# Moving the heads' beta products to VectorE, the convolutions one block later, and the last weight forms one block earlier in a one-core decoder layer

## The chip, the cores and the metric

The kernel runs on one NeuronCore of a Trainium2 chip. The metric is device time in microseconds (us) of one execution, and lower is better. TensorE (PE) multiplies matrices, VectorE (DVE) and ScalarE (ACT) work on elements, GpSimd (POOL) does some elementwise work and issues the stores that the code calls `store`, and SyncE (SP) issues all other transfers.

## The reference

One layer on x of shape 1 x 1024 x 1024 (sequence by channels), all in float32, with a conditioning vector c that gives shift, scale and gate:

```python
h = rmsnorm(x, pre_mix_g) * (1 + sc1) + sh1
glu_in, qkv, gates = split(h @ w_in)
# branch A: u = u_val * sigmoid(u_gate); causal depthwise conv of 31 taps over 512 channels;
#           layernorm, silu, projection
# branch B: stick-breaking attention, 8 heads of 64
z = q @ k.T / 8
log_keep = where(causal, log_sigmoid(-z), 0)
log_after = reverse_cumsum(log_keep) - log_keep
a = where(causal, exp(log_sigmoid(z) + log_after), 0);  o = a @ v
y = (sigmoid(g_conv) * y_conv + sigmoid(g_att) * y_att) @ w_o
x = x + ga1 * rmsnorm(y, post_mix_g)
h = rmsnorm(x, pre_ffn_g) * (1 + sc2) + sh2
gate, up = split(h @ w_ffn_in);  y = (silu(gate) * up) @ w_ffn_out      # 2816 wide
x = x + ga2 * rmsnorm(y, post_ffn_g)
```

## The kernel before

**Layout.** Activations lie with the channels on the 128 partitions. A float32 product is made of three fast ones: each operand is split into a rounded part hi and a rest lo, and hi*hi, hi*lo and lo*hi are added in PSUM. So every operand costs one copy on ScalarE (L158) and one subtraction on VectorE.

**Order.** The program's text gives each instruction a priority. A planner walks a clock of its own costs and puts the ready instruction of the best priority next on its engine; `tc.high_priority(offset=n)` moves a block n places ahead, a negative offset moves it back. On the chip each engine takes its instructions in the order so fixed. Tiles come from pools with a number of buffers for each tag, and a new tile waits until the buffer's last tile is done with, a store that reads it included. Pools open on a stack: a pool that opens after another has closed lies on the same memory, and its tiles wait for the tiles that lay there.

**The mixing stage.** For p = 0 to 3 the text has `glu(p)` (the gate and value products of 128 convolution channels; their product u is written to DRAM as `v_d`), `conv(p)` and `attend(p)` (heads 2p and 2p+1). `conv(p)` reads `v_d` back in another arrangement into `ph` (one buffer), loads five 512 KB tiles `cvw` of weights into the three `wraw` buffers that all raw weights share, and makes 80 products of 128 x 128 by 128 columns (L361). Before this change `conv(3)` stands behind the loop, together with the gate products that are left. `attend(p)` has high priority; `qk_pair(p+1)`, the next heads' queries and keys, stands between its two heads. So TensorE fills the gaps of the heads with whatever stands behind them in the text and has its data.

**A head** takes 12 steps. One step: scores z on TensorE (L451, L452, and L454 for the mask); two sigmoids on ScalarE, kap of -z (L455) and beta of z (L456); a running product over kap from the right on VectorE (L459); beta times the running product on GpSimd (L461); then the 128 x 128 blocks are transposed on TensorE (L471), split by ScalarE (L474) and VectorE (L475), and multiplied with v (L480, L481). Over 8 heads there are 96 steps, 48 of them 512 wide and 16 each of 384, 256 and 128.

**The FFN's first half** runs over 22 column blocks f in a pool `pv`, with tags `y2` (8 buffers of 4 KB a partition) and `wt` (9 of 2 KB). A block has seven products of 12 matmuls each on TensorE; for f under EARLY = 11 two of them were made earlier. Its results go out with two stores from `y2` tiles to `g_d` (names p and uw). For f in W2_AT, `w2_forms` also makes sums of four quarters of a second-half weight, splits them, and stores them to `w_d`: four loads, four sums and four rests on VectorE, four copies on ScalarE, four `y2` tiles and four 512 KB stores on GpSimd's queue.

**The FFN's second half** opens `pg` on the memory where `pv` lay. Its tag `gt` (5 buffers) holds the split operands of the first sweep `pa`: ScalarE's copy of X (L158, gb) writes into such a buffer, and TensorE's first products (L1397) read it.

Of the kernel before, what the change touches and what calls it, by code (L numbers as in the profile page):

```python
# [10 lines left out]
F32 = mybir.dt.float32  # L11
# [3 lines left out]
ALU = mybir.AluOpType  # L15
# [3 lines left out]
P = 128  # L19
# [3 lines left out]
CH = 512  # L23
# [27 lines left out]
EARLY = 11  # L51
TLATER = 40
CORDER = [(0, 1, 2, 3)] * 6 + [(3, 2, 1, 0)] * 2
FH = FT // 2
# [3 lines left out]
AHEAD = 2  # L58
FIN_AT = (8, 8)
DOT_AT = "pb"  # L60
W2_AT = tuple(range(EARLY, EARLY + FH))
W2_LATER = 100
W_S3, W_S1, W_S2, W_S4 = range(4)

# [10 lines left out]
def tile_block(ctx: ExitStack, tc: tile.TileContext, xT, vecs, crow, ada1, ada2, win, wv, wcv, wat, wo, w1, w2, cvw, out):  # L75
    nc = tc.nc
    act, dve, pool, pe = nc.scalar, nc.vector, nc.gpsimd, nc.tensor

    def mkpool(stack, name, bufs=1, **kw):
        return stack.enter_context(tc.tile_pool(name=name, bufs=bufs, reuse_waits="tile", **kw))  # L80
# [21 lines left out]
    def load(dst, src):  # L102
        nc.sync.dma_start(dst, src)
# [85 lines left out]
    def bank(name):  # L189
        return psm.tile([P, CH], F32, tag="main", name=name)  # L190
# [6 lines left out]
    with ExitStack() as s0:  # L197
# [48 lines left out]
        with tc.high_priority(offset=2 * SOONER):  # L246
            for c in range(NCH):
                m, a = (p0.tile([P, CH], F32, tag="nr", name=f"nr{c}{i}", bufs=4) for i in range(2))
# [69 lines left out]
    with ExitStack() as sC:  # L318
        pc = mkpool(sC, "pc")
        with ExitStack() as sA:  # L320
# [25 lines left out]
            def conv(ct):  # L346
                ph = pc.tile([P, NG, SH - 1 + TM], F32, tag="ph", name=f"ph{ct}", bufs=1)
                pool.memset(ph[:, :, 0:SH - 1], 0.0)
                load(ph[:, :, SH - 1:], v_d[ct].rearrange("g p m -> p g m"))
                wts = []  # L350
                for hf in range(2):
                    cv = bank(f"pcv{ct}_{hf}")
                    o = sgp.tile([P, NG // 2, TM], F32, tag="sg", name=f"co{ct}_{hf}", bufs=2)
                    for gi in range(NG // 2):
                        g = hf * (NG // 2) + gi
                        for d in range(SH):
                            n, at = divmod((g * SH + d) * P, T)
                            if n == len(wts):
                                wts.append(wp.tile([P, T], F32, tag="wraw", name=f"cvw{ct}_{n}"))
                                load(wts[n], cvw[ct, n])  # L360
                            pe.matmul(cv[:, gi * TM:(gi + 1) * TM], wts[n][:, at:at + P],  # L361
                                      ph[:, g, SH - 1 - d:SH - 1 - d + TM], start=(d == 0), stop=(d == SH - 1))
                    for gi in range(NG // 2):
                        b = C_CB + ct * NG + hf * (NG // 2) + gi
                        act.activation(o[:, gi], cv[:, gi * TM:(gi + 1) * TM], AF.Identity, bias=vec[:, b:b + 1],
                                       scale=1.0)
                    load(u_d[ct][hf * (NG // 2):(hf + 1) * (NG // 2)].rearrange("g p m -> p g m"), o)
# [54 lines left out]
            def head(p, hh, qst, kst, klo, vts, oT):  # L422
# [3 lines left out]
                tag = f"{p}_{hh}"  # L426
                av = None
                order = CORDER[2 * p + hh]
                for ci, c in enumerate(order):
                    if ci % 2 == 0:  # L430
                        av = psv.tile([P, CH], F32, tag="av", name=f"av{tag}_{c}")
                    avc = av[:, (c % 2) * 256:(c % 2) * 256 + 256]
                    kaps = {}
                    nsc = 1 if c < 2 else 2
                    for sc in range(nsc - 1, -1, -1):
                        probs = []
                        for i in (2 * c, 2 * c + 1):
                            W = P * (i + 1)
                            if i not in kaps:
                                kaps[i] = pa.tile([P, T], F32, tag="kap", name=f"ka{tag}_{i}", bufs=2)  # L440
                            kap = kaps[i]
                            s_lo, s_hi = sc * CH, min(W, (sc + 1) * CH)
                            w = s_hi - s_lo
                            beta = pa.tile([P, CH], F32, tag="beta", name=f"be{tag}_{i}_{sc}", bufs=4)
                            tcols = slice(i * P, (i + 1) * P)
                            z = psz.tile([P, CH], F32, tag="z", name=f"z{tag}_{i}_{sc}")
                            z_lo = s_lo if w >= 256 else max(0, s_hi - 256)
                            z_hi = max(s_hi, z_lo + 256)
                            zw, zo = z_hi - z_lo, s_lo - z_lo
                            diag = s_hi == W  # L450
                            pe.matmul(z[:, :zw], qst[:, tcols], kst[:, z_lo:z_hi], start=True, stop=False)  # L451
                            pe.matmul(z[:, :zw], qst[:, tcols], klo[:, z_lo:z_hi], start=False, stop=not diag)  # L452
                            if diag:
                                pe.matmul(z[:, zo + w - P:zo + w], identb, mask, start=False, stop=True)  # L454
                            act.activation(kap[:, s_lo:s_hi], z[:, zo:zo + w], AF.Sigmoid, bias=0.0, scale=-0.125)  # L455
                            act.activation(beta[:, :w], z[:, zo:zo + w], AF.Sigmoid, bias=0.0, scale=0.125)  # L456
                            rev = kap[:, s_lo:s_hi][:, ::-1]
                            init = 1.0 if diag else kap[:, s_hi:s_hi + 1]
                            dve.tensor_tensor_scan(rev, rev, rev, init, op0=ALU.mult, op1=ALU.bypass)  # L459
                            m = w - 1 if diag else w  # L460
                            pool.tensor_tensor(beta[:, :m], beta[:, :m], kap[:, s_lo + 1:s_lo + 1 + m], op=ALU.mult)  # L461
                            probs.append(beta)
                        for jp in range(min(c, 2 * sc + 1), 2 * sc - 1, -1):
                            tr = pst.tile([P, CH], F32, tag="tr", name=f"tr{tag}_{c}_{jp}")
                            for jj in range(2):
                                j = 2 * jp + jj
                                for ii in range(2):
                                    jo = (j - 4 * sc) * P
                                    src = zeros if (jp == c and jj == 1 and ii == 0) else probs[ii][:, jo:jo + P]
                                    o = jj * 256 + ii * P  # L470
                                    pe.transpose(tr[:, o:o + P], src, ident)  # L471
                            ahi = pa.tile([P, CH], F32R, tag="ahi", name=f"ahi{tag}_{c}_{jp}", bufs=2)
                            alo = pa.tile([P, CH], F32R, tag="alo", name=f"alo{tag}_{c}_{jp}", bufs=2)
                            act.activation(ahi, tr, AF.Copy)  # L474
                            dve.tensor_tensor(alo, tr, ahi, op=ALU.subtract)  # L475
                            for jj in range(2):
                                j = 2 * jp + jj
                                lhs = vts[j][:, hidx].rearrange("p a d -> p (a d)")
                                cols = slice(jj * 256, jj * 256 + 256)
                                pe.matmul(avc, lhs, ahi[:, cols], start=(jp == c and jj == 0), stop=False)  # L480
                                pe.matmul(avc, lhs, alo[:, cols], start=False, stop=(jp == 0 and jj == 1))  # L481
                    if ci % 2 == 1:
                        cs = slice((c // 2) * CH, (c // 2 + 1) * CH)
                        act.activation(oT[half, cs], av[other], AF.Copy)
                        dve.tensor_tensor(oT[half, cs], av[half], oT[half, cs], op=ALU.add)
# [16 lines left out]
            for p in range(4):  # L502
                glu(p)
                if p == 2:
                    v = v_half(1)
                if p < 3:
                    conv(p)
                qk = attend(p, qk, v)
            conv(3)
            for n in PLAIN:  # L510
# [21 lines left out]
    with ExitStack() as sG:  # L532
        pg = mkpool(sG, "pg")
# [228 lines left out]
    with ExitStack() as sF:  # L762
# [592 lines left out]
        for f in range(PIN, FT):  # L1355
            raw_w(f)
            for _ in ffn(f):
                pass
            if f in W2_AT:
                with tc.high_priority(offset=-W2_LATER):  # L1360
                    w2_forms(W2_AT.index(f))

    with ExitStack() as sG:
        pg = mkpool(sG, "pg")
        psg = mkpool(sG, "psg", 4, space=PSUM)

# [4 lines left out]
            return hp.tile([P, 2, CH], dt, tag="act", name=name)  # L1371

        def x_tile(name):
            return pg.tile([P, 2, CH], F32, tag="xr", name=name, bufs=4)

        def bank(name):
            return psg.tile([P, CH], F32, tag="main", name=name)
# [175 lines left out]
        c22 = out_tiles("c22", (h_tile, g_tile))  # L1553
        b2 = sweep("pa", prep1, (True, True))
        c11 = out_tiles("c11", (x_tile, x_tile))
        for n in range(NH):
            act.activation(c11[n], ka[n], AF.Copy)
# [131 lines left out]
```

## Time and profile before

| | |
|---|---|
| median of 3 runs (lowest to highest) | 1438.71 us (1438.03 to 1440.59) |
| the profiled execution: its own time | 1440.23 us |
| its span in the trace | 1438.2 us |
| TensorE busy | 1384.5 us, 96% of the span |
| VectorE busy | 1020.9 us, 71% |
| ScalarE busy | 653.8 us, 45% |
| GpSimd busy | 195.4 us, 14% |
| mean DMA rate | 180 GB/s |

Busy is time with at least one instruction in the engine. Matmuls overlap one another, so a stage in which TensorE is shown as fully busy can still differ in how many matmuls it gets done; the counts tell that.

### The profile page before, as it was taken

The numbers are of one execution on the slowest core, as the hardware profiler recorded it, in microseconds if no ns is written. First come the engines' busy times: TensorE is split into PE (matmuls) and PEld (weight loads), VectorE is DVE, ScalarE is ACT, GpSimd is POOL, SyncE is SP. The second block draws the span as 40 slices with busy tenths as digits, with TensorE's granted clock in tenths as the row PEclk, the third lists the DMA queues.
The fourth block names the chain that finished last, engine by engine and source line by source line (L and its number), as shares of the span: only waits on it lengthen the run. The fifth ranks groups of instructions, "written<-read, shape, count | busy, mean of one in ns | idle before, by whom it ended". The sixth has DMA issues, their size and how long they took to land.

```text
span 1438.2 us, 18913 instructions
## 1 busy us (share of the span) xinstructions
PE 1384.5 (96%) x6882; PEld 1159.7 (81%) x6882; DVE 1020.9 (71%) x1496; ACT 653.8 (45%) x1136; POOL 195.4 (14%) x279
## 2 busy tenths in 40 slices
PE   4999999999999999999999999999999998999996
PEld 4888888898888777788877778888888886888886
DVE  7686466546576789779579878777787786785357
ACT  6275456436463447413356543333444443433441
POOL 0033042412230111000011100001111111000000
PEclk9999999999999999999999999999999999999998
DMA  9211304113043563784934535445677789588833
GB/s 382 88 45 59 132 30 147 44 60 118 22 156 103 192 210 126 274 300 142 359 117 160 185 138 179 158 146 180 221 259 252 238 285 393 182 316 294 282 120 117
DMA packets 91260, 259.25 MB, mean 180 GB/s; under 512 B 9760, under 2 KB 20128, under 8 KB 90144
## 3 DMA queue, kind: packets, MB, share of 16 engines
q1 hardware_dynamic: 75232, 203.52, 41.3%
q0 software_dynamic: 15936, 54.54, 10.1%
q8 instruction: 54, 0.88, 0.2%
q14 instruction: 38, 0.31, 0.1%
HBM read 191.43 MB, written 66.58 MB: 179 GB/s over the span
## 4 chain that ended last, share of the span: by engine, by line
PE 52%; issue 26%; DMA 7%; DVE 7%; POOL 4%; ACT 2%; SPq 0%; POOLq 0%; DVEq 0%; ACTq 0%
PE ka L1397 8%; PE pwo L790 6%; PE pb L1397 4%; PE pg L179 3%; PE pgv L179 3%; PE pv L381 3%; PE pcv L361 3%; PE pgg L179 2%; PE pq L179 2%; PE pk L179 2%; PE pa L1397 2%; PE tr L471 2%; PE ka L315 2%; POOL w_d L106 2%; POOL g_d L106 2%
## 5 line engine op out<-in xcount | busy, mean ns | idle before, releaser
L461 POOL TENSOR_TENSOR be<-be,ka 128x127 f32<-128x127 f32 (+2 forms) x96 | 99.9, 1053 | 234.1 <-DVE ka L459 120.5
L459 DVE TENSOR_TENSOR_SCAN ka<-ka 128x128 f32<-128x128 f32 (+2 forms) x96 | 95.2, 1015 | 40.1 <-ACT ka L455 40.0
L475 DVE TENSOR_TENSOR alo<-tr,ahi 128x512 fp32r<-128x512 f32 x80 | 53.3, 684 | 43.8 <-ACT ahi L474 43.3
L455 ACT ACTIVATE ka<-z 128x128 f32<-128x128 f32 (+2 forms) x96 | 47.7, 498 | 55.2 <-PE z L454 36.3
L474 ACT ACTIVATE ahi<-tr 128x512 fp32r<-128x512 f32 x80 | 46.5, 603 | 44.3 <-PE tr L471 32.0
L1397 PE MATMUL ka<-gt,w2f 128*128 128x512 f32 x264 | 63.4, 389 | 0.7 <-DMA w2f<-w_d 0.7
L1397 PEld LDWEIGHTS ka<-gt,w2f 128*128 128x128 f32 x264 | 49.5, 188 | 11.3 <-issue 1.0
L975 PE MATMUL ke<-b,w_hi 128*128 128x512 f32 x176 | 55.1, 394 | 0.0
L134 DVE SCALAR_TENSOR_TENSOR ada<-ada,cb 128x1024 f32<-128x1024 f32 x32 | 38.9, 1222 | 19.3 <-DMA ada<-in_ada_dram 19.2
L456 ACT ACTIVATE be<-z 128x128 f32<-128x128 f32 (+2 forms) x96 | 47.3, 501 | 6.0 <-PE tr L471 5.9
L471 PE MATMUL tr<-ident,be 128*128 128x128 f32 x288 | 49.2, 273 | 0.7 <-DVE alo L475 0.4
L480 PE MATMUL av<-ahi,vst 128*128 128x256 f32 x160 | 44.7, 294 | 1.9 <-ACT be L456 1.2
L481 PE MATMUL av<-alo,vst 128*128 128x256 f32 x160 | 43.2, 296 | 2.1 <-DVE alo L475 1.9
L106 POOL DMA_DIRECT2D g_d<-uw x22 | 11.9, 542 | 245.0 <-DVE uw L1288 245.0
L361 PE MATMUL pcv<-ph,cvw 128*128 128x128 f32 x320 | 42.8, 276 | 1.2 <-DMA ph<-v_d 1.2
L361 PEld LDWEIGHTS pcv<-ph,cvw 128*128 128x128 f32 x320 | 39.7, 192 | 2.1 <-DMA ph<-v_d 1.1
L1397 PE MATMUL ka<-gb,wa 128*128 128x512 f32 x132 | 33.0, 398 | 6.8 <-ACT gb L158 6.8
L975 PEld LDWEIGHTS ke<-b,w_hi 128*128 128x128 f32 x176 | 33.0, 188 | 7.7 <-issue 1.0
L381 PE MATMUL pv<-wv_hi,hhi 128*128 128x256 f32 x128 | 37.1, 290 | 1.4 <-DVE qst L405 0.8
L158 ACT ACTIVATE gt<-X 128x512 fp32r<-128x512 f32 x33 | 20.4, 629 | 38.9 <-PE ka L1397 11.6
L471 PEld LDWEIGHTS tr<-ident,be 128*128 128x128 f32 x288 | 35.0, 140 | 2.6 <-POOL be L461 1.1
L381 PE MATMUL pv<-wv_hi,hlo 128*128 128x256 f32 x128 | 36.5, 285 | 0.0
(525 smaller groups left out, 4128.8 us busy)
## 6 DMA issues: line engine op xcount, KB each, us to landing
w_d<-w2o POOLq DMA_DIRECT2D x44, 512.0 KB, 7.5
w2f<-w_d SPq DMA_DIRECT2D x44, 512.0 KB, 5.4
ada<-in_ada_dram SPq DMA_DIRECT2D x32, 512.0 KB, 5.4
w2r<-in_w_dram SPq DMA_DIRECT2D x44, 256.0 KB, 3.9
w1g<-in_w_dram SPq DMA_DIRECT2D x21, 512.0 KB, 3.6
w1u<-in_w_dram SPq DMA_DIRECT2D x21, 512.0 KB, 4.7
cvw<-in_cvw_dram SPq DMA_DIRECT2D x20, 512.0 KB, 3.6
ada_w<-in_ada_dram SPq DMA_DIRECT2D x8, 1024.0 KB, 12.7
```

The costliest lines, as they stand in the source:

```text
L106: nc.gpsimd.dma_start(dst, src)
L179: pe.matmul(bank, st[:, cols], mv[k][:, c * CH:(c + 1) * CH], start=(i == 0 and s == 0), stop=(i == n - 1 and s == 2))
L361: pe.matmul(cv[:, gi * TM:(gi + 1) * TM], wts[n][:, at:at + P], ph[:, g, SH - 1 - d:SH - 1 - d + TM], start=(d == 0), stop=(d == SH - 1))
L381: pe.matmul(pv[:, :256], st[k][:, tcols], mv[:, wc], start=(k == 0 and i == 0), stop=(k == KT - 1 and i == 2))
L455: act.activation(kap[:, s_lo:s_hi], z[:, zo:zo + w], AF.Sigmoid, bias=0.0, scale=-0.125)
L459: dve.tensor_tensor_scan(rev, rev, rev, init, op0=ALU.mult, op1=ALU.bypass)
L461: pool.tensor_tensor(beta[:, :m], beta[:, :m], kap[:, s_lo + 1:s_lo + 1 + m], op=ALU.mult)
L471: pe.transpose(tr[:, o:o + P], src, ident)
L475: dve.tensor_tensor(alo, tr, ahi, op=ALU.subtract)
L790: pe.matmul(bank_, st[:, cols], mv[k][:, cs], start=(k == 0 and q == 0), stop=(k == KT - 1 and q == 2))
L975: pe.matmul(kbs[f], wes[f][st][:, cols], t[:, mv], start=(i == 0 and j == 0 and q == 0), stop=(j == HK - 1 and q == 2), skip_group_check=i ...
L1397: pe.matmul(dst, w[st][:, cols], g[mv], start=first and s == 0, stop=last and s == 2, skip_group_check=more)
```

## The change

There are three edits. Beta's product moves from `pool` to `dve`. `conv(p)` for p below 3 moves from beside the heads of its own block to beside those of the next, so that `conv(2)` stands with the last pair of heads and `conv(3)` still behind the loop. At the FFN's border `w2_forms` runs for f = 10 to 20 in place of 11 to 21, and the tag `xr` (4 buffers of 4 KB a partition, used from the end of the first sweep on) gets a pool `px` of its own, which opens ahead of `pg`.

```diff
-W2_AT = tuple(range(EARLY, EARLY + FH))
+W2_AT = tuple(range(EARLY - 1, EARLY - 1 + FH))
...
-                            pool.tensor_tensor(beta[:, :m], beta[:, :m], kap[:, s_lo + 1:s_lo + 1 + m], op=ALU.mult)
+                            dve.tensor_tensor(beta[:, :m], beta[:, :m], kap[:, s_lo + 1:s_lo + 1 + m], op=ALU.mult)
...
                 glu(p)
                 if p == 2:
                     v = v_half(1)
-                if p < 3:
-                    conv(p)
+                if p:
+                    conv(p - 1)
                 qk = attend(p, qk, v)
             conv(3)
...
     with ExitStack() as sG:
+        px = mkpool(sG, "px")
         pg = mkpool(sG, "pg")
...
         def x_tile(name):
-            return pg.tile([P, 2, CH], F32, tag="xr", name=name, bufs=4)
+            return px.tile([P, 2, CH], F32, tag="xr", name=name, bufs=4)
```

## Rows read from the trace of the kernel before

**Rows 1.** The page's first two parts: engines, and TensorE in 40 slices.

```profile
PE 1384.5 (96%) x6882; PEld 1159.7 (81%) x6882; DVE 1020.9 (71%) x1496; ACT 653.8 (45%) x1136; POOL 195.4 (14%) x279
...
PE   4999999999999999999999999999999998999996
...
PEclk9999999999999999999999999999999999999998
```

**Rows 2.** TensorE's waits over the whole span: total, times, longest.

```profile
PE pvar L245 <- DVE rstd L238: 17.7, 1, 17.7
PE ka L1397 <- ACT gb L158: 6.8, 1, 6.8
...
PE av L481 <- DVE alo L475: 1.9, 2, 1.5
...
PE pcv L361 <- DMA ph<-v_d: 1.2, 2, 0.9
```

**Rows 3.** Stretches around the FFN's border: busy us by engine, clock, DMA.

```profile
core 0: us, PE busy (x) PEld busy (x) DVE busy (x) ACT busy (x) POOL busy (x), PEclk, DMA share, GB/s
...
960.00:1000.00 40.00, 40.00 (x178) 33.13 (x177) 30.93 (x50) 14.11 (x24) 3.23 (x6) 1.00 0.47 154
1160.00:1200.00 40.00, 40.00 (x178) 33.14 (x177) 30.79 (x49) 19.34 (x35) 6.45 (x12) 1.00 0.91 326
1180.00:1225.00 45.00, 38.24 (x162) 31.14 (x161) 29.53 (x47) 17.54 (x32) 4.32 (x8) 0.92 1.04 394
1200.00:1240.00 40.00, 33.24 (x140) 27.00 (x139) 27.09 (x44) 14.97 (x27) 1.09 (x2) 0.91 0.85 319
```

**Rows 4.** The chain of waits across the border, 1194 to 1212 us.

```profile
1194.63 12.30 DMA w_d<-w2o
...
1207.01 0.64 ACT gb L158
1207.64 0.04 issue
1207.69 2.08 PE ka L1397 x4
```

**Rows 5.** Stretches of the mixing stage, columns as in rows 3.

```profile
60.00:480.00 420.00, 412.67 (x2526) 360.49 (x2525) 261.05 (x332) 221.57 (x451) 111.03 (x112) 1.00 0.26 83
120.00:140.00 20.00, 18.19 (x123) 15.49 (x122) 15.68 (x19) 12.24 (x25) 8.70 (x8) 1.00 0.19 64
200.00:220.00 20.00, 18.62 (x135) 16.56 (x134) 15.45 (x20) 12.43 (x28) 8.91 (x9) 1.00 0.25 79
380.00:400.00 20.00, 17.34 (x111) 14.72 (x110) 13.37 (x18) 10.78 (x26) 7.56 (x9) 1.00 0.15 52
82.00:138.00 56.00, 53.52 (x377) 47.50 (x376) 41.53 (x54) 33.43 (x77) 23.17 (x23) 1.00 0.09 29
365.00:425.00 60.00, 57.28 (x374) 50.25 (x373) 41.53 (x50) 36.21 (x81) 23.43 (x23) 1.00 0.28 94
```

**Rows 6.** The chain of waits at the first convolution.

```profile
129.45 2.61 DMA v_d<-u
...
132.12 3.94 DMA ph<-v_d
136.05 0.14 issue
136.19 2.25 PE pcv L361 x18
```

**Rows 7.** SP's issues behind that store, in order of time.

```profile
138.24 3.04 SPq L103 DMA_DIRECT2D cvw<-in_cvw_dram  x2
...
144.44 0.41 SPq L103 DMA_DIRECT2D wq_raw<-in_win_dram  x1
```

**Rows 8.** Groups by shape: beta's product on POOL, VectorE's nearest products.

```profile
L461 POOL TENSOR_TENSOR be<-be,ka 128x512 f32<-128x512 f32 x32 | 42.3, 1335 | 70.8 <-ACT be L456 40.8 <-DVE ka L459 21.7 <-ACT ahi L474 2.5
...
L1288 DVE TENSOR_TENSOR uw<-uw 128x512 f32<-128x512 f32 x22 | 15.1, 687 | 1.6 <-ACT uw L1287 1.2
```

**Rows 9.** The last stores of the FFN's first half, GpSimd's queue.

```profile
1192.82 2.34 POOL L106 DMA_DIRECT2D w_d<-w2o  x4 [4.16 <-DVE w2o L878]
1200.62 0.54 POOL L106 DMA_DIRECT2D g_d<-uw  x1 [5.46 <-DVE uw L1288]
1201.95 0.55 POOL L106 DMA_DIRECT2D g_d<-p  x1 [0.78 <-DVE p L1296]
```

**Rows 10.** Stores between 1150 and 1220 us: KB each, median us to landing.

```profile
w_d<-w2o POOLq DMA_DIRECT2D x12, 512.0 KB, 8.4
...
g_d<-p POOLq DMA_DIRECT2D x4, 256.0 KB, 5.2
```

**Rows 11.** ScalarE's copies of the sweep's weights, from the timeline.

```profile
1223.34 0.63 ACT L158 ACTIVATE wa<-wa 128x512 fp32r<-128x512 f32 x1 [4.78 <-DMA wa<-in_w_dram]
```

## The prediction

> **What bounds the kernel now.** I read the page's engine table first: TensorE is busy 96% of the span, and in the 40 slices only the first, the last and one near the five-sixths mark fall short of 9 [rows 1]. So TensorE's work sets the time, and an edit that leaves that work as it is can win only TensorE's gaps. The list of its waits then says where the gaps are: 17.7 us at the start, which no edit touches, one of 6.8 us at L1397, and then small ones of under 2 us [rows 2]. The change touches two places, and for each I took the stretches around it.
>
> At the FFN's border a full stretch of 40 us holds 178 matmuls; the one from 1200 holds 140, with a granted clock of 0.91 [rows 3]. The chain of waits names the cause: the last `w_d` store takes 12.30 us to land, only then does ScalarE write the first gb, and TensorE starts 0.68 us after that; its first four matmuls take 2.08 us [rows 4], where full stretches need 40/178 = 0.225 us each. So gb's buffer lies on a weight form that is still being stored.
>
> In the mixing stage, from 60 to 480 us, TensorE is idle for 420 - 412.67 = 7.3 us. Three stretches of 20 us hold 1.8 + 1.4 + 2.7 = 5.9 of them [rows 5]. The first is a round trip: u goes to DRAM in 2.61 us, comes back as `ph` in 3.94 us, and the convolution starts 6.7 us after the store did [rows 6]. The second has the same shape. In the third the last pair of heads runs out of other work while `conv(3)` waits for its `ph`.
>
> **The border, part by part.** Removed: `w2_forms` after f = 21. The forms of its weight go out one block earlier, 84 matmuls or 84 x 0.225 = 18.9 us, so that their four stores, issued from 1192.82 on [rows 9], are issued near 1174; with the 12.30 us of [rows 4] the last has landed by about 1190, and TensorE reaches the border at 1201. What is late next: only the last block's two `g_d` stores, issued at 1200.62 and 1201.95 [rows 9], which hold 2 of the 8 `y2` buffers and land about 5.2 us later [rows 10]. With `px` first, `pg` begins 16 KB further on, so that `gt`'s five buffers lie on the upper four `y2` buffers and on `wt` tiles, which nothing stores. An operand that lies on such a `g_d` tile comes free near 1201.95 + 0.55 + 5.2 = 1207.7. If it is one of the later of the five, this costs nothing or little, as one operand serves 12 matmuls, or 2.7 us. I take the whole gap as gone: 178 - 140 = 38 matmuls at 0.225 us, -8.5 us; this has both the idle 6.8 us and the slow matmuls behind it. Bounds: 0 (the first operand lies on a `g_d` tile) and -8.5.
>
> The Trainium skill (Trace Analysis, section Identifying the Most-Contended Engine) calls busy matmul time a bad measure of what TensorE has left and wants the weight loads' busy share. By it the border costs 40 x (1 - 27.00/33.14) = 7.4 us [rows 3], against 8.5 us by the count; I keep the count.
>
> Added: a form block at f = 10, which has five products in place of seven, 60 x 0.225 = 13.5 us. VectorE works 30.93 of 40 us there [rows 3], 10.4 us in such a block, and the form adds eight instructions of about 0.69 us (by the nearest shape [rows 8]), 5.5 us: 2.4 us more than the block has. The form has the lower priority and the next block, of 18.9 us, has 18.9 x (1 - 30.79/40) = 4.4 us free with its own form counted in, so I take 0; uncovered it is +2.4 us.
>
> The transfers: from 1180 to 1225 the DMA engines are full, at 394 GB/s [rows 3], and the sweep's weights are late, with ScalarE waiting 4.78 us for one until 1223.34 [rows 11]. That one serves the fifth step; at 24 matmuls a step TensorE would want it near 1201 + 4 x 5.4 = 1222.6, some 8 us sooner than now. But the four stores of 0.52 MB leave this stretch, 2.1/0.394 = 5.3 us of it, so it lands near 1218, and with a copy and a rest (1.3 us) it is ready with 3 us to spare. Price 0; if the stores don't move out of the way, about +2 to +3 us.
>
> **Beta on VectorE.** POOL loses 96 products; 32 of them, 512 wide, take 1.335 us each [rows 8]. VectorE gains them. Its nearest row is the product of two SBUF tiles of that width, 0.687 us [rows 8]. Upper bound: 96 x 0.687 = 66 us. Lower: by columns, the mean width being 383, 96 x 0.687 x 383/512 = 49 us. I take 55, since narrow instructions keep some of their fixed time. All of it lies beside TensorE's work: VectorE is busy 261 of the 420 us [rows 5], and 316 still fits. A pair of heads gains 24 products, 12 to 16.5 us; in the two tightest stretches VectorE has 56 - 41.5 = 14.5 and 60 - 41.5 = 18.5 us free [rows 5]. That is close in the first. A step gets shorter by a handover and by about 1.3 - 0.7 = 0.6 us. On TensorE's path I take 0.
>
> The Trainium skill (VectorE: DVE Perf Modes, section on the trn2 errata) gives a float32 tensor_tensor of N columns (N + 151)/0.96 ns, a fixed cost per instruction that speaks against 96 more of them; by it an estimate is 54 us. Its 691 ns at 512 agrees with the row's 687; no row here has the narrow widths on VectorE.
>
> **The convolutions.** Nothing is added: per block one `ph` load, five `cvw` loads, two `u_d` stores and 80 matmuls move behind `glu(p+1)`. On SP's queue the `cvw` loads no longer stand ahead of the next query weights, which today are issued at 144.44, behind the first convolution's waits [rows 7]; so the query and key products can fill the first pair of heads at once, and each later pair finds a convolution whose `ph` can have been there for long. Of the 5.9 us in the three stretches, I take -4. Bounds: -7.3 (all of the stage's idle time), and a loss: `conv(3)` now follows `conv(2)` directly with one `ph` buffer, so its load of 3.94 us [rows 6] can start only when `conv(2)` is through. The heads that are left and the transfer's start hide it, else +3.9 us.
>
> **Sum.** -8.5 - 4 = -12.5 us against the profiled execution's own 1440.23 us (span 1438.2, 2.0 around it): 1427.7. That execution lies 1.5 us above the median shown, so the median to expect is 1426.2, say 1426.
>
> **The rivals.**
> (a) Likeliest, as above, chance 0.55. Its own range takes the convolutions from -7.3 to 0: 1423 to 1430.
> (b) The border wins, the mixing stage doesn't: the `ph` handover or VectorE's longer queue gives back what the round trips cost, net up to +3.9. Around 1433. Speaking for it: one `ph` buffer, and VectorE 78% busy in 120 to 140 before the products come. Chance 0.15.
> (c) The first gb lies on a late `g_d` tile: it comes at 1207.7 in place of 1206.9, nothing is won there, and -4 is left: 1434.7. Against it: two late buffers of eight, and `px` moves the first operands' place. Chance 0.13.
> (d) The wait goes and a transfer takes its place, +3 at the sweep's fifth step: 1429. Chance 0.05.
> (e) Slower: VectorE becomes the heads' bound. Place: the four pairs of heads. It decides if the free time of a pair can't be used because the running products and the splits wait in order for ScalarE. If half of it is usable, the tight pairs lack 16.5 - 7.2 and 16.5 - 9.2 us, 17 in all, and TensorE stands for it once its other work is out: 1438.7 - 8.5 + 17 = 1447. Against it: TensorE has other work for most of that time. Chance 0.07.
> (f) The planner's new order puts as many waits elsewhere as it takes away, about 1438.7. Chance 0.05.
>
> **How the numbers follow.** About 0.2% (2.9 us) is what a measurement of this kernel can tell from no change. Faster means below 1435.8: (a), (b), (d) and nearly half of (c), 0.81. Same: the rest of (c) and (f), 0.12. Slower: (e), 0.07. The range runs from 1420, the full 7.3 us in the mixing stage and some 3 us by a better order behind it, to 1437, the upper side of (c); above lie (e) and (f).
>
> **What would show it.** Right: no wait of L1397 on gb near 1190 to 1210, a full 178 matmuls in each 40 us there and a granted clock of 1.00; L461 on DVE at 0.5 to 0.7 us; L361 with no wait on `ph`; 4 us less idle from 60 to 480. Wrong: gb waiting on a `g_d` store; TensorE waiting on VectorE's running product or beta's product in the heads; a wait on `ph` between `conv(2)` and `conv(3)`.

## The result, and the profile after

The changed kernel takes 1420.48 us (median of 4 runs, 1418.78 to 1421.85) against 1439.28 us before, a ratio of 0.987 with a 95% interval of 0.9854 to 0.9885: 18.8 us less. That is faster, as forecast, but 5.5 us below the forecast of 1426: outside the 1423 to 1430 of rival (a) and just inside the lower end of the whole range, 1420. The profiled execution took 1418.78 us, with a span of 1417.0 us.

The page's engines and slices after, with the group of beta's product:

```profile
PE 1376.3 (97%) x6882; PEld 1155.8 (82%) x6882; DVE 1061.4 (75%) x1592; ACT 653.0 (46%) x1136; POOL 96.3 (7%) x183
...
PE   4999999999999999999999999999999999999996
...
PEclk8999999999999999999999999999999999999999
...
L461 DVE TENSOR_TENSOR be<-be,ka 128x127 f32<-128x127 f32 (+2 forms) x96 | 53.3, 572 | 9.7 <-ACT be L456 5.0
```

The gap near the five-sixths mark [rows 1] is gone. TensorE's number of matmuls is the same, POOL has lost 96 instructions and VectorE has gained them: 53.3 us of busy time in all. VectorE's own busy time rose by less, from 1020.9 to 1061.4 us. In part its instructions overlap, and in part others became shorter: the running products of 128 columns (L459) took 541 ns on average before and 418 after. TensorE's waits after (total, times, longest):

```profile
PE pvar L245 <- DVE rstd L238: 17.0, 1, 17.0
...
PE ka L1398 <- ACT gb L158: 1.2, 1, 1.2
...
PE pcv L361 <- DMA ph<-v_d: 0.9, 1, 0.9
```

L1397 of before is L1398 here, as the pool `px` adds a line. Its wait on gb has shrunk from 6.8 us [rows 2] to 1.2 us. The chain of waits across the border after:

```profile
1184.72 2.73 PE ka L867 x12
...
1187.48 0.02 ACT wa L158
...
1188.02 0.62 ACT gb L158
...
1188.68 1.19 PE ka L1398 x4
```

No store stands in it any more, where before the chain ran through a 12.30 us store [rows 4]. After TensorE's last product of the first half ScalarE makes one copy of a weight (wa) and then gb:

```profile
1187.48 0.63 ACT L158 ACTIVATE wa<-wa 128x512 fp32r<-128x512 f32 x1 [1.36 <-PE ka L867]
1188.02 2.70 ACT L158 ACTIVATE gb<-X 128x512 fp32r<-128x512 f32 x5
```

The sweep's first four matmuls take 1.19 us in place of 2.08. Two 40 us stretches at the border after (columns as in [rows 3]):

```profile
1160.00:1200.00 40.00, 38.76 (x172) 31.77 (x171) 26.89 (x43) 16.87 (x30) 4.30 (x8) 1.00 1.00 371
...
1200.00:1240.00 40.00, 40.00 (x178) 33.15 (x177) 28.16 (x44) 15.74 (x27) 0.00 (x0) 1.00 0.57 199
```

The granted clock stays at 1.00, the upper level of 2.4 GHz, after an idle time of 1.2 us; before it was 0.91 over 40 us after 6.8 us idle [rows 3]. The stretch behind the border holds its full 178 matmuls. The mixing stage after:

```profile
60.00:480.00 420.00, 417.36 (x2559) 366.16 (x2558) 309.29 (x438) 224.96 (x457) 13.02 (x18) 1.00 0.28 90
120.00:140.00 20.00, 20.00 (x113) 16.93 (x111) 17.51 (x24) 11.75 (x22) 0.00 (x0) 1.00 0.25 80
200.00:220.00 20.00, 20.00 (x132) 17.61 (x130) 18.09 (x25) 13.90 (x29) 0.12 (x1) 1.00 0.65 202
380.00:400.00 20.00, 18.78 (x154) 17.44 (x153) 17.62 (x28) 13.20 (x32) 0.12 (x1) 1.00 0.61 192
```

The first two stretches that held gaps [rows 5] are full. From 60 to 480 us TensorE idles 2.6 us in place of 7.3.

To see where the 18.8 us came from I used four marks of TensorE that every version has: the first `pv` (values), the last of the plain gate products `pg`, the first `pwo` (output projection) and the first `pa` (the sweep). Their lines in the tile views give the first and the last start; before:

```profile
L381 PE MATMUL pv<-wv_hi,hhi x128: 277/283/386, 73.8 to 314.0; 128*128 128x256 f32 x128
...
L179 PE MATMUL pg<-hhi,wg_lo x64: 387/389/478, 420.5 to 468.0; 128*128 128x512 f32 x64
...
L790 PE MATMUL pwo<-mhi,wo_hi x88: 388/389/798, 679.5 to 740.0; 128*128 128x512 f32 x88
...
L1397 PE MATMUL pa<-gb,wa x132: 389/389/628, 1209.6 to 1269.2; 128*128 128x512 f32 x132
```

and after:

```profile
L381 PE MATMUL pv<-wv_hi,hhi x128: 274/283/384, 71.7 to 297.2; 128*128 128x256 f32 x128
...
L179 PE MATMUL pg<-hhi,wg_lo x64: 388/390/398, 413.3 to 458.6; 128*128 128x512 f32 x64
...
L790 PE MATMUL pwo<-mhi,wo_hi x88: 388/390/799, 666.6 to 728.1; 128*128 128x512 f32 x88
...
L1398 PE MATMUL pa<-gb,wa x132: 388/390/395, 1189.7 to 1248.4; 128*128 128x512 f32 x132
```

The differences, with those of the experiments below (one profiled execution each, us):

| kernel | first pv | pv to last pg (heads) | pg to first pwo (gates) | pwo to first pa (FFN to sweep) |
|---|---|---|---|---|
| before | 73.8 | 394.2 | 211.5 | 530.1 |
| whole change | 71.7 | 386.9 | 208.0 | 523.1 |
| whole change again (e11) | 71.5 | 386.8 | 207.9 | 523.2 |
| border alone (e1) | 72.7 | 394.9 | 211.2 | 525.4 |
| forms alone (e2) | 71.0 | 394.2 | 212.3 | 531.8 |
| px alone (e3) | 73.2 | 395.2 | 210.8 | 523.8 |
| both mixing edits (e4) | 72.1 | 386.8 | 208.4 | 528.2 |
| convolutions alone (e5) | 73.0 | 387.8 | 212.3 | 530.0 |
| beta alone (e6) | 73.2 | 396.8 | 207.9 | 528.1 |
| whole change, beta twice (e7) | 73.2 | 387.9 | 211.2 | 522.9 |
| whole change, two buffers for ph (e8) | 70.9 | 385.2 | 208.1 | 524.3 |
| gate loads alone (e9) | 74.0 | 394.7 | 211.6 | 529.5 |
| whole change and gate loads (e10) | 73.8 | 386.9 | 210.9 | 524.8 |

Of the span's 21.2 us the first 2.1 is the start of the layer, which no edit touches (e10 has the whole change and starts at 73.8, so this is scatter between executions). The heads give 7.3, the gates 3.5, and the border 7.0, with another 0.9 in the sweep itself (first to last `pa`: 59.6 us before, 58.7 after). The heads' column is steady: 394.2 to 395.2 in the five versions whose mixing stage is that of before, 386.8 to 386.9 in the four with both mixing edits and nothing else there.

Could the marks only show work that was moved across them? TensorE's busy time and count between the first two marks answer that (columns as in [rows 3]); in order before, the whole change, the convolutions alone (e5) and beta alone (e6):

```profile
73.80:468.00 394.20, 387.62 (x2415) 340.03 (x2416) 246.45 (x312) 208.97 (x430) 108.34 (x107) 1.00 0.25 83
...
71.70:458.60 386.90, 385.01 (x2416) 339.65 (x2417) 286.93 (x405) 207.71 (x428) 9.26 (x11) 1.00 0.26 85
...
73.00:460.80 387.80, 385.15 (x2415) 339.73 (x2416) 249.00 (x314) 210.27 (x432) 110.25 (x108) 1.00 0.26 85
...
73.20:470.00 396.80, 388.16 (x2415) 340.37 (x2416) 279.60 (x397) 206.10 (x425) 8.54 (x11) 1.00 0.26 83
```

All four hold the same 2415 matmuls, or one more. So the heads' 7.3 us are won on the same work: 4.7 us are idle time (6.6 to 1.9), and 2.6 us are time that is shown as busy (387.62 to 385.01).

### The profile page after: what moved, and what is told of

It is laid out like the page before. It is cut to its first block, busy times and chain, and to the rows that moved or that the text cites. A ratio compares the mean times of both kernels' runs of the same rounds, so it can differ in the third digit from the quotient of the medians.

```text
span 1417.0 us, 18795 instructions
## 1 busy us (share of the span) xinstructions
PE 1376.3 (97%) x6882; PEld 1155.8 (82%) x6882; DVE 1061.4 (75%) x1592; ACT 653.0 (46%) x1136; POOL 96.3 (7%) x183
## 4 chain that ended last, share of the span: by engine, by line
PE 89%; DVE 5%; DMA 3%; ACT 2%; issue 1%; SPq 0%; DVEq 0%; ACTq 0%; POOLq 0%
PE ka L867 14%; PE ka L1398 8%; PE kc L867 8%; PE pwo L790 5%; PE pb L1398 4%; PE pgv L179 3%; PE pg L179 3%; PE pyc L179 3%; PE pya L179 3%; PE pv L381 3%; PE pcv L361 3%; PE ka L315 2%; PE tr L471 2%; PE ke L975 2%; PE pq L179 2%; PE pgg L179 2%
## 5 line engine op out<-in xcount | busy, mean ns | idle before, releaser
L459 DVE TENSOR_TENSOR_SCAN ka<-ka 128x128 f32<-128x128 f32 (+2 forms) x96 | 91.3, 968 | 22.9 <-ACT ka L455 22.6
L1398 PE MATMUL ka<-gt,w2f 128*128 128x512 f32 x264 | 63.4, 390 | 0.2 <-DMA w2f<-w_d 0.2
L461 DVE TENSOR_TENSOR be<-be,ka 128x127 f32<-128x127 f32 (+2 forms) x96 | 53.3, 572 | 9.7 <-ACT be L456 5.0
L1398 PEld LDWEIGHTS ka<-gt,w2f 128*128 128x128 f32 x264 | 49.5, 188 | 10.9 <-issue 0.6
L158 ACT ACTIVATE s1o<-s 128x512 fp32r<-128x512 f32 x22 | 13.8, 629 | 50.5 <-PE ka L867 39.1
L381 PE MATMUL pv<-wv_lo,hhi 128*128 128x256 f32 x128 | 36.4, 286 | 0.0
L451 PE MATMUL z<-kst,qst 128*128 128x256 f32 (+2 forms) x96 | 36.3, 383 | 0.0
```

The lines of the kernel that those rows point to most:

```text
L381: pe.matmul(pv[:, :256], st[k][:, tcols], mv[:, wc], start=(k == 0 and i == 0), stop=(k == KT - 1 and i == 2))
L461: dve.tensor_tensor(beta[:, :m], beta[:, :m], kap[:, s_lo + 1:s_lo + 1 + m], op=ALU.mult)
L1398: pe.matmul(dst, w[st][:, cols], g[mv], start=first and s == 0, stop=last and s == 2, skip_group_check=more)
```

## The experiments

**The border's two edits, alone and together.** My theory was that the first gb lies on a weight form's tile, and that the place and the earlier forms together free it; the rival (c) was that it lies on the last block's own store.

e1, the forms one block earlier and `px`, nothing else:

```diff
-W2_AT = tuple(range(EARLY, EARLY + FH))
+W2_AT = tuple(range(EARLY - 1, EARLY - 1 + FH))
...
+        px = mkpool(sG, "px")
...
-            return pg.tile([P, 2, CH], F32, tag="xr", name=name, bufs=4)
+            return px.tile([P, 2, CH], F32, tag="xr", name=name, bufs=4)
```

> Only the border's two edits: weight forms one block earlier, and the pool of its own for xr. My theory, by the step of the changed kernel's trace from the last FFN product to the first product of the sweep (gap 6.8 to 1.2 us) and the slow matmuls behind it (about 1.9 us): 7 to 8 us under the kernel before, ratio about 0.995, nothing else moved. Rival, that the border's gain needs the new order of the mixing stage too: under 3 us.

Measured: 1432.04 us against 1439.81, ratio 0.9948 (0.9931 to 0.9965), 7.8 us less. The wait on gb is 1.2 us and the mixing stage is that of before.

e2, only the forms one block earlier:

```diff
-W2_AT = tuple(range(EARLY, EARLY + FH))
+W2_AT = tuple(range(EARLY - 1, EARLY - 1 + FH))
```

> Only the weight forms one block earlier; xr stays in the second half's pool, which then begins where it did. Theory A, that the wait goes because the last weight form is stored 19 us sooner: the same 7 to 8 us gain as with both edits. Theory B, that the place counts, the first gb then lying on a tile of the last block's own late store: the wait stays, now for a g_d store that is issued about 1 us after the last product and takes some 5 us; gain 0 to 2 us.

Measured: 1442.33 us, ratio 1.0018 (1.0006 to 1.003), so no gain, and 2.5 us more by the medians: the wait of theory B, at more than its price. Its chain of waits at the border:

```profile
1200.79 5.91 DMA g_d<-p
...
1206.77 0.64 ACT gb L158
1207.41 0.04 issue
1207.45 2.07 PE ka L1397 x4
```

The forms' stores are out of the chain, and what is late next is the last block's store of p, just as rival (c) has it, at nearly the same time as [rows 4]. The wait on gb is 7.7 us here, 0.9 more than before; the other 1.6 us are not explained. Moving a late store away is worth nothing while the next store on the same tiles is as late.

e3, only `px`:

```diff
+        px = mkpool(sG, "px")
...
-            return pg.tile([P, 2, CH], F32, tag="xr", name=name, bufs=4)
+            return px.tile([P, 2, CH], F32, tag="xr", name=name, bufs=4)
```

> Only the pool of its own for xr, which moves the first operands 16 KB further on; the forms stay in the last block. Theory A (the forms' time decides): the wait for the last weight form's store stays for some of the five operands, and TensorE stops at the second or third of them; gain under 3 us. Theory B (the first operand's place decides): the first gb is free at once, the operands that lie on a form's earlier stores are needed 5 us later, and 5 to 8 us are gained.

Measured: 1434.09 us, ratio 0.9959 (0.9945 to 0.9973), 5.7 us less. The wait on gb is 1.2 us although the forms still go out as late as before. So the place of the first operands ends the wait, as theory B has it; what the earlier forms add (7.8 against 5.7) lies inside the two intervals.

**The mixing stage's two edits, together and alone.**

e4, beta's product on VectorE and the convolutions moved:

```diff
-                            pool.tensor_tensor(beta[:, :m], beta[:, :m], kap[:, s_lo + 1:s_lo + 1 + m], op=ALU.mult)
+                            dve.tensor_tensor(beta[:, :m], beta[:, :m], kap[:, s_lo + 1:s_lo + 1 + m], op=ALU.mult)
...
-                if p < 3:
-                    conv(p)
+                if p:
+                    conv(p - 1)
```

> Only beta's product on VectorE and the convolutions one block later; the border as before. My theory: the border's gap of 6.8 us and the granted clock of about 0.91 behind it are there again, and the mixing stage gives what it gave in the changed kernel's trace, 7 us from 60 to 480 us and some 3 us in the gate products behind it: 9 to 12 us under the kernel before, ratio about 0.992 to 0.993. Rival, that half of these 10 us is the scatter of single profiled executions: 4 to 6 us.

Measured: 1425.36 us, ratio 0.9898 (0.9881 to 0.9915), 14.5 us less, more than any theory had. The wait on gb is still there, 5.5 us.

e5, the convolutions alone:

```diff
-                if p < 3:
-                    conv(p)
+                if p:
+                    conv(p - 1)
```

> Only the convolutions one block later; beta stays on GpSimd, the border as before. My theory: the round trips of v_d through DRAM are what the mixing stage loses, so the stretches at 120 to 140 and 200 to 220 us are full, and most of the mixing stage's 10 us gain of the two edits together is here: 6 to 10 us under the kernel before. Rival, that the shorter step of a head brings the gain: 0 to 3 us here.

Measured: 1433.99 us against 1438.84, ratio 0.9968 (0.9957 to 0.9979), 4.9 us less. Its stretches of the mixing stage:

```profile
60.00:480.00 420.00, 416.60 (x2555) 365.46 (x2554) 265.64 (x337) 224.20 (x455) 113.49 (x114) 1.00 0.27 88
...
120.00:140.00 20.00, 20.00 (x113) 16.98 (x113) 15.27 (x17) 11.69 (x23) 7.83 (x6) 1.00 0.23 79
200.00:220.00 20.00, 20.00 (x138) 17.81 (x137) 16.51 (x19) 15.72 (x35) 8.26 (x8) 1.00 0.66 216
```

The gaps of the two round trips are gone with this edit alone. The gain lies between my theory (6 to 10) and the rival (0 to 3). By the marks this edit alone brings 6.4 of the heads' 7.3 us, 3.9 of them idle time (6.6 to 2.7) and 2.5 busy time; the gates behind take 0.8 us longer here.

e6, beta's product alone:

```diff
-                            pool.tensor_tensor(beta[:, :m], beta[:, :m], kap[:, s_lo + 1:s_lo + 1 + m], op=ALU.mult)
+                            dve.tensor_tensor(beta[:, :m], beta[:, :m], kap[:, s_lo + 1:s_lo + 1 + m], op=ALU.mult)
```

> Only beta's product on VectorE; convolutions and border as before. My theory: the round trips stay (about 5 us of gaps near 131, 211 and 396 us), VectorE's added 53 us lie beside TensorE's work, gain 0 to 3 us. Rival, that the shorter step brings the gain: 6 us or more. Rival, that VectorE's queue delays other work: slower by 2 us or more.

Measured: 1435.87 us, ratio 0.9981 (0.9972 to 0.9989), 3.0 us less. The same stretches, and below them the waits that grew:

```profile
60.00:480.00 420.00, 410.61 (x2515) 358.63 (x2515) 292.25 (x414) 216.74 (x442) 10.15 (x14) 1.00 0.26 82
...
120.00:140.00 20.00, 17.38 (x122) 15.31 (x121) 17.08 (x25) 11.32 (x24) 0.00 (x0) 1.00 0.23 79
200.00:220.00 20.00, 17.36 (x125) 15.11 (x124) 18.35 (x29) 12.16 (x28) 0.00 (x0) 1.00 0.24 79
```

```profile
PE av L481 <- DVE alo L475: 3.8, 4, 1.5
PE pcv L361 <- DMA ph<-v_d: 2.4, 3, 1.1
```

Here the gaps are larger than before (2.6 us in each of the two, against 1.8 and 1.4 [rows 5]). In the heads this edit by itself loses 2.6 us (394.2 to 396.8 in the table), and wins 3.6 in the gates and 2.0 from there to the sweep. With the convolutions moved as well, the heads' loss is gone: both edits give 7.4 us there, where their sum would be 6.4 - 2.6 = 3.8. So the parts don't add up: 4.9 and 3.0 us alone, 14.5 together. Of that surplus of 6.6 us the marks show 3.6 in the heads and 0.3 in the gates; the rest, 2.7 us, is about what the intervals of the three ratios allow (1.6, 1.2 and 2.4 us to each side), and stays open.

**Does VectorE have room?** e7, the whole change with every beta product made a second time into a spare tile, so that VectorE gets the added work twice:

```diff
+                            spare = pa.tile([P, CH], F32, tag="spare", name=f"sp{tag}_{i}_{sc}", bufs=1)
+                            dve.tensor_tensor(spare[:, :m], beta[:, :m], kap[:, s_lo + 1:s_lo + 1 + m], op=ALU.mult)
                             dve.tensor_tensor(beta[:, :m], beta[:, :m], kap[:, s_lo + 1:s_lo + 1 + m], op=ALU.mult)
```

> The changed kernel with each beta product made twice on VectorE, once into a spare tile that nothing reads; the output is the same. VectorE gets another 53 us in the heads. My theory, that VectorE has room and TensorE's total work decides: 0 to 4 us over the changed kernel, about 1420 to 1425 us. Rival, that VectorE is already the heads' bound after the change: 15 to 40 us over it, with TensorE waiting on L459, L461 or L475.

Measured: 1424.34 us, ratio 0.9896 (0.988 to 0.9913), 3.9 us above the changed kernel's median, the upper end of my theory.

```profile
60.00:480.00 420.00, 417.06 (x2554) 365.78 (x2554) 346.08 (x522) 222.76 (x451) 12.56 (x18) 1.00 0.27 88
...
380.00:400.00 20.00, 18.49 (x154) 17.39 (x152) 19.83 (x32) 12.05 (x30) 0.12 (x1) 1.00 0.60 194
```

VectorE is busy 346 of 420 us, and 19.83 of 20 in the tightest stretch, and TensorE still idles only 2.9 us over the stage. Another 37 us of busy time on VectorE (346.08 against 309.29) cost some 4, and by the marks only 1.0 of them in the heads (387.9 against 386.9); 3.2 come in the gates, on which more below. Rival (e), with VectorE as the heads' bound, falls.

**What is left.** e8, the whole change with two buffers for `ph` and, at the border, X's operands split ahead of the sweep's weights in the text:

```diff
-                ph = pc.tile([P, NG, SH - 1 + TM], F32, tag="ph", name=f"ph{ct}", bufs=1)
+                ph = pc.tile([P, NG, SH - 1 + TM], F32, tag="ph", name=f"ph{ct}", bufs=2)
...
-            return [(wop2(f"wa11_{j}", w[:, 0], act, dve), op2(f"gb11_{j}", x[:, 0], act, dve)),
-                    (wop2(f"wa12_{j}", w[:, 1], act, dve), op2(f"gb21_{j}", x[:, 1], act, dve))]
+            g11, g21 = op2(f"gb11_{j}", x[:, 0], act, dve), op2(f"gb21_{j}", x[:, 1], act, dve)
+            return [(wop2(f"wa11_{j}", w[:, 0], act, dve), g11), (wop2(f"wa12_{j}", w[:, 1], act, dve), g21)]
```

> The changed kernel with the first sweep's operands of X split ahead of its weights on ScalarE and VectorE, and two buffers for ph. By the changed kernel's trace the first takes up to 1.2 us of TensorE's wait on gb at the border, the second up to 1.0 us of its wait on ph near 396 us: 1 to 2 us under the changed kernel, ratio to the kernel before about 0.986. Rival, that another order of ScalarE's copies moves the wait to the weights: no gain or slower.

Measured: 1420.38 us, ratio 0.9872 (0.9856 to 0.9888), the same as the changed kernel, where I expected 1 to 2 us less. The wait on `ph` is gone and the stretch from 380 to 400 us is full (20.00), but the wait on gb is still 1.2 us. The 0.9 us can't be seen in the time (by the marks the heads are 1.7 us shorter, the way to the sweep 1.2 longer), and the order in the text doesn't move gb: on ScalarE the same copy of wa still stands ahead of it.

**The gates.** In the execution before, the second weight half of the first gate pair was issued behind a load of `ga` that waited for a store, and I took this for the gates' gain of 3.5 us. e9 puts the `ga` loads behind the weights in the kernel before, e10 does so in the changed one, and e11 is the whole change again on the same chip:

```diff
-            load(wu, win[21 + 2 * i])
+            lw = nc.sync.dma_start(wu, win[21 + 2 * i])
...
-            load(p1s[i], e_d0[i])
+            with tc.issue_after(lw.ins):
+                load(p1s[i], e_d0[i])
```

> None of the change's edits: the kernel before, with the loads ga of the gate stage issued right behind the second weight half (gw0b, gw1b and so on) of their pair. Only the order on SP's queue differs, and two small swaps on VectorE and ScalarE. Theory A (part of the gain over the forecast comes from the gate stage, whose first ka product waits for gw0b, which stood on SP behind a load of ga that waits for a store): from 480 to 600 us the idle time of 4.3 to 4.5 us falls to about 2, and the time by 2 to 3 us, to a ratio near 0.998. Rival B (another wait right behind takes its place, and the gain there was the early end of the heads itself): idle time stays above 4 us, time within 1 us of before.

> The whole change with the same reordering of the gate stage's loads on SP. Theory A: the changed kernel has these weights in time already, so the idle time from 480 to 600 us stays near 1.8 us and the time within 1 us of the whole change. Rival B makes no difference here either; a gain of over 2 us would say that the loads were still late in the changed kernel.

> The whole change once more, beside the other two on one chip, so that the reordering of the loads can be read against it: ratio 0.985 to 0.9885, border gap 1.2 us.

Measured: e9 1438.53 us against 1438.82, ratio 0.9995 (0.9984 to 1.0005); e10 1420.08, 0.9869 (0.9851 to 0.9887); e11 1419.91, 0.9871 (0.9853 to 0.9889). Two stretches of the gate stage, 20 to 30 us and 50 to 60 us behind the last `pg`; before:

```profile
488.00:498.00 10.00, 8.40 (x36) 6.35 (x35) 5.70 (x9) 3.10 (x6) 1.07 (x2) 1.00 0.71 254
...
518.00:528.00 10.00, 8.47 (x36) 6.26 (x35) 10.00 (x18) 5.78 (x10) 1.08 (x2) 1.00 0.37 128
```

and in e9:

```profile
488.70:498.70 10.00, 10.00 (x46) 8.29 (x45) 6.99 (x12) 3.54 (x6) 1.07 (x2) 1.00 0.65 231
518.70:528.70 10.00, 7.74 (x26) 5.49 (x26) 10.00 (x18) 5.58 (x10) 1.08 (x2) 0.84 0.32 107
```

The first gap is gone, as I wanted. But in the second one TensorE waits longer, the granted clock is 0.84 there, and 26 matmuls are done in place of 36. From the last `pg` to the first `pwo` the idle time falls only from 4.5 to 3.6 us, and the busy time grows by 1.0 us for the same work. So the time is unchanged, as rival B has it, and my theory falls, though the idle time is not above B's 4 us.

What the gates' 3.5 us hang on is settled in part:

```profile
468.00:679.50 211.50, 207.01 (x899) 167.83 (x898) 172.41 (x253) 91.96 (x127) 17.25 (x32) 1.00 0.61 211
...
458.60:666.60 208.00, 206.23 (x899) 167.90 (x898) 172.71 (x255) 91.24 (x128) 17.25 (x32) 1.00 0.63 215
```

Between these two marks all versions run 898 or 899 matmuls. Before, TensorE idles 4.5 us there, after the change 1.8. Over all runs it is 1.6 to 3.6 us with beta on VectorE and 3.6 to 4.5 us with beta on GpSimd; why beta's place matters here was not tested. The shorter gates (207.9 to 208.4 us) show in e4, e6, e8, e11 and the changed kernel, which have beta on VectorE, and in none with beta on GpSimd. But e7 (211.2) and e10 (210.9) have beta on VectorE too. In both the granted clock falls in one stretch of the stage, to 0.83 over 10 us in e7 and to 0.88 in e10; e10's stretch and the same one of e11:

```profile
510.70:520.70 10.00, 8.00 (x29) 5.76 (x28) 10.00 (x18) 5.65 (x10) 1.08 (x2) 0.88 0.30 107
...
508.30:518.30 10.00, 8.64 (x37) 6.38 (x37) 10.00 (x18) 5.98 (x11) 1.08 (x2) 1.00 0.29 106
```

TensorE idles 2.0 us in the one and 1.4 in the other, and the next twelve matmuls take 4.61 us in e10 and 3.02 in e11. Of the 3.0 us by which e10's gates are longer than e11's, 2.1 are such busy time (208.44 against 206.33) and 0.9 idle time. So a part of what the gates gain or lose is whether the clock falls at one of the stage's gaps, and one profiled execution each doesn't tell how often it does.

## Why the prediction was right, and where its sizes were off

**The border, -8.5 us: right.** The wait was on a buffer that a store still read, and `px` removed it. By medians the border alone measured 7.8 us (5.0 to 9.9); in the profiled pair it is 7.0 up to the sweep and 0.9 in it. The step that was too neat is "I take the whole gap as gone": 1.2 us of it remain, as gb stands on ScalarE behind a copy wa that comes only after TensorE's last ka. The code shows why: wa goes into the `whi` and `wlo` buffers, three of each, that the weights of the FFN's products use too, and each of the last three copies of wa starts when such a product ends (the last at 1187.48, behind the ka that ends at 1187.45). The remaining wait is these two copies, wa and gb. By the Trainium skill (Perfetto Trace Analysis, section Identifying the Most-Contended Engine), the border's cost, weighed by the weight loads' busy share, was estimated at 7.4 us. Here e1's time agrees with either figure within its interval.

**The forms a block earlier, and rival (c).** The prediction gave the gain to both edits together and asked which tile the first operand lies on. e2 and e3 answer: without `px` it lies on the last block's store, which takes 5.91 us from its issue to land, where rival (c) had 0.55 + 5.2 (it lands at 1206.70, not 1207.7, in an execution that reaches the first pwo 2.0 us sooner); with `px` it doesn't. Rival (c) is the right mechanism for the change without `px`. That the forms had to go out earlier for the gain was not shown: `px` alone ends the wait.

**The form block at f = 10, 0 us, and the transfers, 0 us: right as far as can be told.** From the first pwo to the first pa the border alone takes 1.6 us more than `px` alone (525.4 against 523.8), but the whole change takes 523.1 and 523.2, and e7, e8 and e10, which have both border edits too, 522.9 to 524.8: a difference of that size is scatter. TensorE waits for no weight of the sweep, and 1200 to 1240 us is full: rival (d) falls.

**Beta on VectorE, 55 us of work and 0 on the path: the work is right, the path was mis-sized.** The 96 products take 53.3 us of busy time, 51.8 in e6. By the Trainium skill (VectorE: DVE Perf Modes, section on the trn2 errata) the estimate over the mix of widths is 53.4 us (the prediction's 54 is rounded too high), which the trace bears out. On TensorE's path the edit alone costs 2.6 us in the heads and takes 3.6 off the gates, 3.0 us less by medians; the stretch from the first pwo to the sweep, which it doesn't touch, is 2.0 us shorter too. On top of the moved convolutions it takes 1.0 us off the heads (387.8 to 386.8).

**The convolutions, -4 us: right for the idle time, too small for the time.** It is the main miss. The convolutions alone took 3.9 us of idle time off the heads, just what the term says, but 6.4 us of time; both edits gave 7.3 us there, and 3.5 came in the gates. The step that failed is the premise that such an edit "can win only TensorE's gaps", and with it the bound "-7.3 (all of the stage's idle time)". 2.6 of the heads' 7.3 us came in stretches that are shown as busy, for the same 2415 matmuls. That the heads gave just the 7.3 us of the bound is luck: 4.7 us of it were idle time. The gates' 3.5 us were allowed for only as "some 3 us by a better order behind it" at the end of the range, without a mechanism. And the two edits were worth more together than one by one: e6's rows show that with beta's product on VectorE alone the gaps are larger where the convolution isn't ready, and e5's that the moved convolutions fill just these stretches. The feared second wait on the single `ph` buffer, at most 3.9 us, came to 0.9 us.

**The sum.** Forecast -8.5 - 4 = -12.5; in the profiled pair -7.9 at the border and in the sweep and -10.8 from the first pv to the first pwo, together -18.7, beside 18.8 by the medians. That the measured time still lies in the range is owed to its wide lower end. Of the signs that the prediction named, the granted clock of 1.00, beta's product at 0.57 us and 4 us less idle time came out; the waits on gb and on `ph` shrank to 1.2 and 0.9 us but did not go. Rivals (b), (e) and (f) didn't happen.

## What to carry to other kernels

When a stage's first write waits on memory that an earlier stage still stores from, changing which tiles lie there is worth more than issuing the late store earlier: the next-latest store takes its place. When an edit shortens a chain that other work fills, and another edit moves that other work, time them together as well as alone; here 4.9 and 3.0 us made 14.5. Idle time is no upper bound of what a better order can win, so compare marks of the work between versions, not only gaps.

## What the runs showed of the hardware that was not expected

A beta product of 512 columns takes 747 ns on VectorE in the changed kernel by the groups by shape, but 689 ns in e6, near the 687 of the nearest row of before [rows 8]:

```profile
L461 DVE TENSOR_TENSOR be<-be,ka 128x512 f32<-128x512 f32 x32 | 23.4, 747 | 4.3 <-ACT be L456 2.1
```

The difference is a single product of 2.60 us; the other 31 come to 687 ns. It begins while GpSimd subtracts two SBUF tiles, and ends 0.55 us after that subtraction:

```profile
256.31 3.03 POOL L168 TENSOR_TENSOR wv_lo<-wv_raw,wv_hi 128x1024 fp32r<-128x1024 f32 x1 [13.89 <-ACT wv_hi L158]
...
257.29 2.60 DVE L461 TENSOR_TENSOR be<-be,ka 128x512 f32<-128x512 f32 x1
```

e4, e8, e10 and e11 show the same pair with the same 2.60 us and 0.55 us, and e7 has its spare product there, with 2.11 us. In e6 no beta product begins during one of these subtractions, and the longest takes 694 ns. So in all six cases the product ended only behind GpSimd's subtraction. How much the products on GpSimd held up VectorE in the kernel before was not measured by itself.

VectorE at 82% of a 420 us stage (346 us in e7) held TensorE up by less than 3 us in that stage. Idle time alone doesn't tell when TensorE's granted clock falls: 2.0 us of it in a 10 us stretch of the gate stage came with 0.88 in e10 and with 1.00 in e6 (580 to 590 us).
